# Attention by pairs of heads in half-height matmuls, inside a one-core transformer trunk kernel

## The chip, the cores and the metric

The kernel runs on one NeuronCore of a Trainium2 chip. TensorE (the matrix engine, PE in the profile; its weight loads are the row PEld), VectorE (DVE), ScalarE (ACT), GpSimd (POOL) and SyncE (SP, which issues DMAs) each follow their own instruction stream and wait for one another through semaphores. The metric is the device time of one execution in microseconds (us); lower is better. The program is launched once for the whole layer.

## What is computed

One layer of a streaming encoder over 1024 tokens of width 1024, in f32. What matters here is its middle part:

```python
z = rmsnorm(x) @ w_in                 # 512 columns u, then q, k, v of 512 each
# 8 heads of 64: every chunk of 64 tokens attends to itself and the 8 chunks before
s  = q @ k.T * (1 / 8) + bias[head]   # relative position, clipped; masked outside the band
pr = softmax(s)
o  = pr @ v
a  = pool_mixer(u)                    # trailing means over 2, 4, 8, 16 tokens, a small linear map
h  = x + concat(a, o) @ w_out
```

After that come a gated MLP of width 2816 with a causal depthwise convolution, a gated embedding, and a last norm. They are not touched by the change.

To keep f32 accuracy with the matrix engine's faster f32r type, an operand is split into a high part (rounded to f32r) and a low part (the rest). A product of two split operands is made of three matmuls: high x high, high x low, low x high. `mm3` (L126 to L130) does this; `split` (L132 to L134) makes the two parts with one copy on ScalarE and one subtract on VectorE.

## The kernel before, in words

Tokens stand in eight tiles of 128. A query tile t sees at most five tiles of keys (t - 4 to t), so a tile's score row has 128 to 640 columns. The stages around attention are: a start (norm, first projections of Q and K for heads 0 and 1, values for the first four heads), the attention stage, the output projection, the MLP, the gate.

In the attention stage one instruction stream of TensorE is written out by hand; the other engines' order is made by the scheduler from priorities (`high_priority(AHEAD)` moves something ahead). The main loop (L549 ff.) runs over 64 items i, head by head, tile by tile:

- `scores(i)` (L341): the 64 rows of a head are stacked twice into the array's 128 rows, high and low part, so that two matmuls (L352 and L353 in two column halves for five key tiles, L360 and L361 otherwise) give all four products. VectorE adds the bias and takes the row minimum (scores are kept negated) out of PSUM (L354 or L362), ScalarE takes the exponential with its sum (L364), VectorE the reciprocal (L365), and the scaling goes to ScalarE for every third item (L367) and to VectorE for the rest (L369). Score rows have three buffers `Sb`.
- `probs_t(i - 2)` (L371): the probabilities of two items ago are transposed in blocks of 128x128 (L378) into PSUM banks 6 and 7 and copied out as high part (ScalarE, L385) and low part (VectorE, L386).
- `values(...)` (L392): for a window of two query tiles, up to 12 matmuls of 256 columns against the values (L395, L396), then two instructions that join the two halves (L401, L402).
- Between these come steps of a generator `fill` (`rest`): projections of the other heads' Q and K (`project_qk`), of the remaining values (`project_v`) and of the pooling part (`project_u`), each step three matmuls of 512 columns or six of 256. There are 32 steps for each of three Q/K pairs, 32 for the values and 64 for the pooling part: 192. `fill_room` decides how many steps follow each item from estimates of the other engines' time (`BASE` and more) and of TensorE's, so that `FILL` steps are spread over the loop.
- `project` (L407) loads a block of weights (a DMA by SP), splits it and multiplies at once. Two weight buffers exist (`wring`).
- `qk_stack` (L274 to L292): for each head six instructions per half of 512 tokens put the projected Q and K (`qk32`) into the stacked layout. They go into a list `later`, of which `LATER` run per item.

Of the kernel before, what the change touches and what calls it, by code (L numbers as in the profile page):

```python
# [11 lines left out]
P = 128  # L12
# [52 lines left out]
FILL = 164  # L65
BASE = 2.0
LATER = 3
DRAIN = 4
# [4 lines left out]
def key_tiles(i):  # L73

    return min(i % NTOK + 1, BANDT) if 0 <= i < N_HEADS * NTOK else 0


def fill_room():


    vec_t, pe_t = [], []
    for i in range(N_HEADS * NTOK):
        a, b = key_tiles(i), key_tiles(i - 2)
        vec_t.append(BASE + 0.2 * key_tiles(i - 3) + 0.13 * b)
        pe_t.append(0.11 * a + 0.11 * b + (0.22 * (key_tiles(i - 5) + 1) if i % 2 and i >= 5 else 0.0))
    lo, hi = 0.0, 10.0
    for _ in range(60):
        m = (lo + hi) / 2
        room = [max(0.0, m * v - p) / 0.65 for v, p in zip(vec_t, pe_t)]
        lo, hi = (m, hi) if sum(room) < FILL else (lo, m)  # L90
    return room


def trunk(tc, xT, pT, vecs, w_qk0, w_in, w_v, bias, counts, pool_w, w_out, w_up, w_down,
# [4 lines left out]
    with tc.tile_pool(name="sb", bufs=1) as sb, \  # L99
# [47 lines left out]
        st = [small[:, 56 + 3 * i:59 + 3 * i] for i in range(3)]  # L147
        sa = [small[:, b:b + 3] for b in (24, 27, 30, 33, 66, 69)]
# [7 lines left out]
        stacks = []  # L156
        for s in range(2):
            base = r(96 + 12 * s, 3072).rearrange("p (a t) -> p a t", a=3)
            stacks.append((base[:, 0], base[:, 1], base[:, 2]))
# [6 lines left out]
        biasb = [f(12 + 2.5 * s, 640) for s in range(2)]  # L166
        Sb = [f(b, 640) for b in (17, 19.5, 57.5)]
# [106 lines left out]
        def qk_stack(j):  # L274

            Q1, K1, K2 = stacks[j]
            a = slice(HD * j, HD * j + HD)
            b = slice(HD * (1 - j), HD * (1 - j) + HD)
            q, k = qk32[0], qk32[1]
            todo = []  # L280
            for h in range(2):
                z = slice(h * 512, (h + 1) * 512)
                todo += [
                    lambda z=z: act.activation(Q1[a, z], q[a, z], AF.Copy, scale=-0.125),
                    lambda z=z: dve.scalar_tensor_tensor(Q1[b, z], q[a, z], -0.125, rv(Q1[a, z]),
                                                         ALU.mult, ALU.subtract),
                    lambda z=z: act.activation(K2[a, z], k[a, z], AF.Copy),
                    lambda z=z: dve.tensor_tensor(K2[b, z], k[a, z], rv(K2[a, z]), ALU.subtract),
                    lambda z=z: act.activation(K1[b, z], k[a, z], AF.Copy),
                    lambda z=z: dve.tensor_copy(K1[a, z], rv(K2[b, z])),  # L290
                ]
            return todo  # L292
# [27 lines left out]
        later += qk_stack(0)  # L320
        run_later(len(later))
        later += qk_stack(1)
# [6 lines left out]
        def load_bias(h):  # L329
            b = biasb[h % 2]  # L330
# [5 lines left out]
        def keys(i):  # L336
            t = i % NTOK
            k0 = max(0, t - 4)
            return i // NTOK, t, k0, t + 1 - k0

        def scores(i):  # L341
            h, t, k0, nk = keys(i)
            Q1, K1, K2 = stacks[h % 2]
            b = biasb[h % 2]
            q = Q1[:, t * P:(t + 1) * P]
            S = Sb[i % 3]
            s_ = st[i % 3]
            n, ki = nk * P, k0 * P
            if nk == BANDT:
                for z in range(2):  # L350
                    ks = slice(ki + 320 * z, ki + 320 * z + 320)
                    pe.matmul(PS[:, 4 + z, 0:320], q, K2[:, ks], start=True, stop=False)  # L352
# [54 lines left out]
        def project(ct, evac, heads=0, eng=dve):  # L407
# [6 lines left out]
            for h in range(2):  # L414
# [5 lines left out]
                while stacked[0] < heads:  # L420
                    yield False
# [900 lines left out]
```

## Time and profile before

| | |
|---|---|
| median of 3 runs | 1134.56 us (1134.21 to 1136.07) |
| the profiled execution's own time | 1134.33 us |
| span of its trace | 1132.6 us |
| TensorE busy | 1123.2 us, 5554 matmuls |
| VectorE busy | 889.3 us |
| ScalarE busy | 600.6 us |
| granted TensorE clock | full in all slices |

The span is the time from the first to the last instruction in the trace; the execution's own time has some 1.7 us around it. In a row of a group (line, engine, operation, out<-in, shape, count) the first number behind the bar is the busy time in us, the second the mean duration of one in ns, the third the idle time of the engine just before them with what ended it. A row of the timeline has start and duration in us. Matmul records overlap, since a matmul starts before the one ahead of it has left the array; their distance from start to start tells what each costs in the stream. A row of the wait view names who waited for whom, with the total in us, the times and the longest.

### The profile page before, as it was taken

How to read it: one execution, taken by the hardware profiler on the slowest of the kernel's cores; microseconds unless marked ns; L12 is line 12 of the kernel's file. 1: busy time of each engine (PE TensorE's matmuls, PEld its weight loads, DVE VectorE, ACT ScalarE, POOL GpSimd, SP SyncE). 2: the span in 40 equal slices, each digit the busy share in tenths (PEclk: the TensorE clock that was granted, in tenths of full speed). 3: DMA queues.
4: the chain of work that ended last, by engine and by line, in shares of the span. 5: the costliest groups of instructions: out<-in, count | busy, mean ns of one | idle time of the engine just before them, and what ended most of it. 6: DMA issues, size and time to landing. Idle time of an engine off the chain costs nothing.

```text
span 1132.6 us, 15484 instructions
## 1 busy us (share of the span) xinstructions
PE 1123.2 (99%) x5554; PEld 948.4 (84%) x5554; DVE 889.3 (79%) x1532; ACT 600.6 (53%) x1056; POOL 143.1 (13%) x188
## 2 busy tenths in 40 slices
PE   9999999999999999999999999999999999999997
PEld 7988998888888888888888888888888888888887
DVE  8678878879658888887788788877877789986845
ACT  8568677765654554444444344444444435564634
POOL 0000000074002210120112011201120112000000
PEclk9999999999999999999999999999999999999999
DMA  7010102104500154575557555765576556420003
GB/s 268 38 49 31 50 12 69 40 29 137 189 19 10 61 148 135 142 174 141 145 153 176 140 143 152 162 157 132 152 160 158 144 149 128 151 93 19 1 27 122
DMA packets 64588, 124.81 MB, mean 110 GB/s; under 512 B 7296, under 2 KB 8704, under 8 KB 64512
## 3 DMA queue, kind: packets, MB, share of 16 engines
q1 hardware_dynamic: 50400, 98.33, 25.9%
q0 software_dynamic: 13824, 25.17, 13.9%
q8 instruction: 43, 0.70, 0.2%
q10 hardware_dynamic: 288, 0.33, 0.1%
q14 instruction: 33, 0.27, 0.1%
HBM read 109.13 MB, written 14.68 MB: 109 GB/s over the span
## 4 chain that ended last, share of the span: by engine, by line
PE 91%; DVE 4%; ACT 2%; issue 1%; POOL 1%; DMA 0%; SPq 0%; POOLq 0%; DVEq 0%; ACTq 0%
PE PS L128 28%; PE PS L129 28%; PE PS L130 28%; PE PS L378 2%; PE PS L396 1%; PE PS L395 1%; DVE R L134 1%; PE PS L353 1%; PE PS L352 1%; ACT R L133 0%; PE PS L361 0%; PE PS L360 0%; ACT F L364 0%; DMA F<-in_xT 0%; POOL TB L786 0%
## 5 line engine op out<-in xcount | busy, mean ns | idle before, releaser
L128 PE MATMUL PS<-R 128*128 128x512 f32 (+1 forms) x1136 | 435.1, 383 | 0.0
L130 PE MATMUL PS<-R 128*128 128x512 f32 (+1 forms) x1136 | 430.6, 379 | 0.0
L129 PE MATMUL PS<-R 128*128 128x512 f32 (+1 forms) x1072 | 412.7, 385 | 0.2 <-DVE R L241 0.2
L130 PEld LDWEIGHTS PS<-R 128*128 128x128 f32 x1136 | 213.5, 188 | 40.7
L128 PEld LDWEIGHTS PS<-R 128*128 128x128 f32 x1136 | 213.7, 188 | 38.8 <-ACT R L133 0.5
L133 ACT ACTIVATE R<-F 128x512 fp32r<-128x512 f32 (+2 forms) x225 | 140.6, 637 | 176.2 <-PE PS L129 77.9
L129 PEld LDWEIGHTS PS<-R 128*128 128x128 f32 x1072 | 201.6, 188 | 38.5 <-DVE R L241 1.3
L134 DVE TENSOR_TENSOR R<-F,R 128x512 fp32r<-128x512 f32 (+2 forms) x221 | 152.3, 700 | 46.7 <-ACT R L133 45.5
L1021 DVE TENSOR_TENSOR F<-F,PS 128x512 f32<-128x512 f32 x140 | 92.6, 681 | 6.8 <-PE PS L130 6.6
L133 ACT ACTIVATE BQ<-RW 128x512 fp32r<-128x512 f32 x90 | 52.6, 622 | 81.6 <-PE PS L129 77.6
L711 DVE TENSOR_TENSOR F<-F 128x512 f32<-128x512 f32 x88 | 60.5, 688 | 37.4 <-DMA F<-in_w_up 36.1
L964 POOL DMA_DIRECT2D RW<-Yd x56 | 49.1, 878 | 255.4 <-DMA RW<-Yd 194.5
L964 POOL DMA_DIRECT2D RW<-in_w_down x40 | 35.5, 949 | 236.3 <-DMA RW<-in_w_down 193.9
L134 DVE TENSOR_TENSOR BQ<-RW,BQ 128x512 fp32r<-128x512 f32 x90 | 59.1, 684 | 2.9 <-PE PS L129 2.2
L364 ACT ACTIVATE F<-F,small 128x640 f32<-128x640 f32 (+2 forms) x64 | 44.4, 693 | 21.5 <-DVE small L362 13.4
L129 PE MATMUL PS<-BQ 128*128 128x512 f32 x140 | 54.6, 390 | 0.1
L130 PE MATMUL PS<-BQ 128*128 128x512 f32 x140 | 54.5, 389 | 0.0
L128 PE MATMUL PS<-R,BQ 128*128 128x512 f32 x140 | 54.5, 389 | 0.0
L129 PE MATMUL PS<-R,BQ 128*128 128x512 f32 x140 | 54.5, 389 | 0.0
L130 PE MATMUL PS<-R,BQ 128*128 128x512 f32 x140 | 54.5, 389 | 0.0
L128 PE MATMUL PS<-BQ 128*128 128x512 f32 x140 | 54.5, 389 | 0.0
L847 ACT ACTIVATE F<-F,vec 128x1024 f32<-128x1024 f32 (+1 forms) x25 | 28.6, 1143 | 43.5 <-DVE F L822 37.2
(188 smaller groups left out, 1797.7 us busy)
## 6 DMA issues: line engine op xcount, KB each, us to landing
F<-in_w_up SPq DMA_DIRECT2D x91, 256.0 KB, 3.8
RW<-Yd SPq DMA_DIRECT2D x60, 256.0 KB, 3.6
RW<-Yd POOLq DMA_DIRECT2D x56, 256.0 KB, 4.7
RW<-in_w_down SPq DMA_DIRECT2D x50, 256.0 KB, 2.9
RW<-in_w_down POOLq DMA_DIRECT2D x40, 256.0 KB, 6.2
Yd<-F SPq DMA_DIRECT2D x40, 256.0 KB, 3.5
F<-in_w_in SPq DMA_DIRECT2D x10, 512.0 KB, 3.5
F<-in_xT SPq DMA_DIRECT2D x16, 256.0 KB, 5.8
```

The lines of the kernel that those rows point to most:

```text
L128: pe.matmul(ps, ahi, bhi, start=first, stop=False, skip_group_check=more)
L129: pe.matmul(ps, ahi, blo, start=False, stop=False, skip_group_check=more)
L130: pe.matmul(ps, alo, bhi, start=False, stop=last, skip_group_check=more)
L133: both = (act.activation(hi, src, AF.Copy), dve.tensor_tensor(lo, src, rv(hi), ALU.subtract))
L134: dve.tensor_tensor(lo, src, rv(hi), ALU.subtract))
L352: pe.matmul(PS[:, 4 + z, 0:320], q, K2[:, ks], start=True, stop=False)
L364: act.activation(S[:, 0:n], S[:, 0:n], AF.Exp, bias=s_[:, 0:1], scale=-1.0, accum_out=s_[:, 1:2])
L378: pe.transpose(pst[:, j * P:(j + 1) * P], S[:, j * P:(j + 1) * P], ident)
L711: return dve.tensor_tensor(rawu[to], rawu[a], rawu[b], op)
L847: act.activation(y, Gb[:, 2 + a:2 + b], AF.Identity, bias=vec[:, C_CB + fi:C_CB + fi + 1], scale=cw(2))
L964: pool.dma_start(t, src, accum_op=ALU.add)
L1021: dve.tensor_tensor(t, t, PS[:, 4 + d], ALU.subtract if n in (1, 5) else ALU.add)
```

## The change

The loop runs over 28 units instead of 64 items: for each of four pairs of heads, tiles 0 and 1 together and then each of the tiles 2 to 7. Q and K of a pair are kept in their natural layout, head 2c in partitions 0 to 63 and head 2c + 1 in 64 to 127, with a high and a low array each (`lay` in place of `qk_stack`); K has two buffers, Q one. Scores are matmuls on 64 rows with a `tile_position` of row 0 or 64, alternating between the two heads and writing to different PSUM banks, three products each (the low x low product of before is no longer formed). A transpose of 128x128 becomes two of 64 rows and 64 moving columns, again one in each half of the rows. Both kinds stand directly together in TensorE's order: `probs_t(u - 1)`, then `scores(u)`; then `values(u - 2)` and the steps of `fill`. Score rows have two buffers, one for each head of the pair. The copies of the transposed probabilities are in two parts where a row has more than three key tiles. The softmax scaling is on ScalarE for the odd heads and on VectorE for the even ones. The weights of the next block are loaded and split when the block before is half done (`weights`). The constants of `fill_room` differ. Cut to its core:

```diff
-FILL = 164
-BASE = 2.0
-LATER = 3
-DRAIN = 4
+FILL = 168
+BASE = 3.0
+LATER = 8
+DRAIN = 9
-def key_tiles(i):
-
-    return min(i % NTOK + 1, BANDT) if 0 <= i < N_HEADS * NTOK else 0
+UNITS = [(c, ts) for c in range(N_HEADS // 2) for ts in [(0, 1)] + [(t,) for t in range(2, NTOK)]]
+NU = len(UNITS)
+PER = NU // (N_HEADS // 2)
+
+
+def key_tiles(u):
+
+    return sum(min(t + 1, BANDT) for t in UNITS[u][1]) if 0 <= u < NU else 0
+
+
+def window_keys(u):
+
+    t = UNITS[u][1][-1] if 0 <= u < NU else 0
+    return min(t + 1, 6) if t % 2 else 0
...
-    for i in range(N_HEADS * NTOK):
-        a, b = key_tiles(i), key_tiles(i - 2)
-        vec_t.append(BASE + 0.2 * key_tiles(i - 3) + 0.13 * b)
-        pe_t.append(0.11 * a + 0.11 * b + (0.22 * (key_tiles(i - 5) + 1) if i % 2 and i >= 5 else 0.0))
+    for u in range(NU):
+        vec_t.append(BASE + 0.5 * key_tiles(u))
+        pe_t.append(0.4 + 0.18 * key_tiles(u) + 0.11 * key_tiles(u - 1) + 0.48 * window_keys(u - 2))
...
-        room = [max(0.0, m * v - p) / 0.65 for v, p in zip(vec_t, pe_t)]
+        room = [max(0.0, m * v - p) / 0.68 for v, p in zip(vec_t, pe_t)]
...
-        stacks = []
-        for s in range(2):
-            base = r(96 + 12 * s, 3072).rearrange("p (a t) -> p a t", a=3)
-            stacks.append((base[:, 0], base[:, 1], base[:, 2]))
+        Q = [r(96 + 4 * x, 1024) for x in range(2)]
+        K = [[r(104 + 8 * s + 4 * x, 1024) for x in range(2)] for s in range(2)]
...
-        biasb = [f(12 + 2.5 * s, 640) for s in range(2)]
-        Sb = [f(b, 640) for b in (17, 19.5, 57.5)]
+        biasb = [f(b, 640) for b in (12, 14.5, 57.5)]
+        Sb = [f(b, 640) for b in (17, 19.5)]
...
+        laid = set()
+
+        def lay(c, x, h):
+
+            laid.add((c, x, h))
+            z = slice(h * 512, (h + 1) * 512)
+            src = qk32[x][:, z]
+            if x:
+                hi, lo = [a[:, z] for a in K[c % 2]]
+                return [lambda: act.activation(hi, src, AF.Copy),
+                        lambda: dve.tensor_tensor(lo, src, rv(hi), ALU.subtract)]
+            hi, lo = [a[:, z] for a in Q]
+            return [lambda: act.activation(hi, src, AF.Copy, scale=-0.125),
+                    lambda: dve.scalar_tensor_tensor(lo, src, -0.125, rv(hi), ALU.mult, ALU.subtract)]
...
-        later += qk_stack(0)
+        for h in range(2):
+            for x in range(2):
+                later += lay(0, x, h)
         run_later(len(later))
-        later += qk_stack(1)
...
+        def softmax(x, b, ps, S, s_):
...
+            if x:
...
+        halves = [slice(HD * x, HD * x + HD) for x in range(2)]
+
+        def scores(u):
+
+            c, ts = UNITS[u]
+            Kh, Kl = K[c % 2]
+            todo = []
+            for z, t in enumerate(ts):
+                ki, nk = max(0, t - 4) * P, min(t + 1, BANDT)
+                n = nk * P
+                wide = n // 2 if nk > 3 else max(n, 256)
+                places = [[4 + x + 2 * (z + y) for y in range(2 if nk > 3 else 1)] for x in range(2)]
+                for i, (q, k) in enumerate(((Q[0], Kh), (Q[0], Kl), (Q[1], Kh))):
+                    for y in range(len(places[0])):
+                        for x in range(2):
+                            pe.matmul(PS[:, places[x][y], 0:wide], q[halves[x], t * P:(t + 1) * P],
+                                      k[halves[x], ki + y * wide:ki + (y + 1) * wide], start=i == 0, stop=i == 2,
+                                      tile_position=(HD * x, 0))
+                for x in range(2):
+                    p0 = places[x][0]
+                    ps = PS[:, p0:p0 + 3:2, 0:wide] if nk > 3 else PS[:, p0, 0:n]
+                    todo.append((x, biasb[(2 * c + x) % 3][:, 640 - n:640], ps, Sb[x][:, z * P:z * P + n],
+                                 st[(4 * u + 2 * z + x) % 8]))
+            return todo
+
+        def probs_t(u):
+
+            c, ts = UNITS[u]
+            total = key_tiles(u)
+
+            def place(x, m):
+                if total < 4:
+                    return (6, 320 + HD * m) if x else (2, HD * m)
+                return (4 + 2 * x, 320 + HD * m) if m < 3 else (2, P * x + HD * (m - 3))
+
+            todo = []
+            for x in range(2):
+                for m in range(total):
+                    bank, col = place(x, m)
+                    for y in range(2):
+                        pe.transpose(PS[:, bank + y, col:col + HD], Sb[x][halves[y], m * P:(m + 1) * P],
+                                     ident[halves[y], halves[y]], tile_position=(HD * y, 0))
+                m = 0
+                for t in ts:
+                    nk = min(t + 1, BANDT)
+                    i0 = max(0, t - 4) - (t // 2 * 2 - 4)
+                    parts = [(0, nk)] if total < 4 else [(0, 3), (3, nk)]
+                    for a, b in parts:
+                        bank, col = place(x, m + a)
+                        todo.append((x, t % 2 * P, i0 + a, i0 + b, PS[:, bank:bank + 2, col:col + HD * (b - a)]))
+                    m += nk
+            return todo
+
+        def probs_out(todo):
+            for x, q, a, b, ps in todo:
+                src = ps.rearrange("p a (k q) -> p a k q", q=HD)
+                hi, lo = [PT[x][:, y, a:b, q:q + P].rearrange("p k (a q) -> p a k q", a=2) for y in range(2)]
+                with tc.high_priority(AHEAD):
+                    act.activation(hi, src, AF.Copy)
+                    dve.tensor_tensor(lo, src, rv(hi), ALU.subtract)
+
+        def values(u):
+            c_, ts = UNITS[u]
+            w = ts[-1] // 2
+            if ts[-1] % 2 == 0:
+                return
+            while c_ >= 2 and len(v_ready) < 2 * w + 2:
+                next(fill)
             ks = list(range(max(0, 2 * w - 4), 2 * w + 2))
...
+            for j in range(2):
+                pt = PT[j]
+                O = PS[:, 2 + j, 256:512]
+                for n_, k in enumerate(ks):
+                    idx = k - (2 * w - 4)
+                    pe.matmul(O, V[:, k, 2 * c_ + j], pt[:, 0, idx], start=n_ == 0, stop=False)
+                    pe.matmul(O, V[:, k, 2 * c_ + j], pt[:, 1, idx], start=False, stop=n_ == len(ks) - 1)
...
-        def project(ct, evac, heads=0, eng=dve):
-            hi, lo = wring[nw[0] % 2]
+        blocks_, ready = [8 + 1, 4 + 1, 8 + 2, 4 + 2, None, 8 + 3, 4 + 3, 2, 3, 0, 1], {}
+
+        def weights(ct):
+
+            if ct is None or ct in ready:
+                return
+            hi, lo = ready[ct] = wring[nw[0] % 2]
             nw[0] += 1
             t = load(w_in[ct]).rearrange("p (k c) -> p k c", k=KT)
             for ks in (slice(0, 4), slice(4, 8)):
-                act.activation(hi[:, ks], t[:, ks], AF.Copy)
-                eng.tensor_tensor(lo[:, ks], t[:, ks], rv(hi[:, ks]), ALU.subtract)
+                split(t[:, ks], hi[:, ks], lo[:, ks])
+
+        def project(ct, evac, wait=None):
+            weights(ct)
+            hi, lo = ready[ct]
+            behind = blocks_[blocks_.index(ct) + 1] if ct != blocks_[-1] else None
             for h in range(2):
                 bankn[0] += 1
                 bank = bankn[0] % 2
                 for k in range(KT):
                     mm3(PS[:, bank], hi[:, k], lo[:, k], XTH[h][:, k], XTL[h][:, k], k == 0, k == KT - 1)
+                    if (h, k) == (1, 0):
+                        weights(behind)
                     yield True
-                while stacked[0] < heads:
-                    yield False
-                if heads:
+                if wait:
+                    while not all((wait[0], x, h) in laid for x in wait[1]):
+                        yield False
                     run_later(len(later))
                 with tc.high_priority(AHEAD):
                     evac(h, PS[:, bank])
...
         def project_qk(p):
-            for c in range(2):
-                yield from project(4 + 4 * c + p, lambda h, ps, c=c: qk_evac(p, c, h, ps), 2 * p)
-            qk_ready.add(p)
+
+            for x in (1, 0):
+                def evac(h, ps, x=x):
+                    qk_out(x, h, ps)
+                    qk_ready.append((p, x, h))
+                yield from project(4 + 4 * x + p, evac, (p - 1, (x,)))
...
-            yield from project(g, evac)
+            yield from project(g, evac, (N_HEADS // 2 - 1, (0, 1)) if g < 2 else None)
...
+
+        def lay_due(u):
+
+            for c, x, h in list(qk_ready):
+                if u >= (c - 1) * PER + (0 if x else PER - 1 if h else 2):
+                    qk_ready.remove((c, x, h))
+                    later.extend(lay(c, x, h))
...
+        for h in range(3):
+            load_bias(h)
+        for u in range(NU + 1):
+            if u < NU:
+                c, ts = UNITS[u]
+                for h in range(2 if ts[-1] > 3 else 1):
+                    while not all((c, x, h) in laid for x in range(2)):
...
+                        lay_due(u - 1)
+                if ts[0] in (0, 4):
+                    run_later(len(later))
+            turned_ = probs_t(u - 1) if u else []
+            sums = scores(u) if u < NU else []
+            if u > 1:
+                values(u - 2)
+            with tc.high_priority(AHEAD):
+                for todo in sums:
+                    softmax(*todo)
+            probs_out(turned_)
+            if u < NU:
+                if u % PER == PER - 1:
+                    for h in (2 * c + 3, 2 * c + 4):
+                        if h < N_HEADS:
+                            load_bias(h)
+                lay_due(u)
+                credit += room[u]
+                while credit >= 1 and next(fill, True) is not False:
+                    credit -= 1
+                    lay_due(u)
+                run_later(LATER)
+        for _ in range(DRAIN):
+            next(fill)
+        values(NU - 1)
```

135 lines of the change are left out of this document (14 added, 121 removed).

## The prediction

> **What bounds the kernel now.** I read the page's sums and slices first, then the wait view of TensorE, then the attention stretch alone (42 to 275 us, from the first score matmul to the last value matmul).
>
> ```profile
> span 1132.6 us, 15484 instructions
> PE 1123.2 (99%) x5554; PEld 948.4 (84%) x5554; DVE 889.3 (79%) x1532; ACT 600.6 (53%) x1056; POOL 143.1 (13%) x188
> ```
>
> ```profile
> 42.00:275.00 233.00, 232.03 (x1472) 206.80 (x1471) 188.66 (x452) 163.81 (x346) 34.91 (x62) 1.00 0.14 43
> ```
>
> ```profile
> PE PS L216 <- DVE B L214: 1.5, 1, 1.5
> PE PS L378 <- DVE B L386: 0.8, 2, 0.5
> ```
>
> The second fence gives the stretch, the busy time with count of PE, PEld, DVE, ACT and POOL, the granted clock (1.00), DMA share and rate. TensorE is busy in 232.03 of 233.00 us there, and its named waits come to about 2.6 us in the whole kernel, of which 0.8 us lie at the transposes (L378). VectorE has 188.66 us of work (81%) and ScalarE 163.81 (70%) in the same stretch. So TensorE's own work sets the time; a change is worth what it takes from or adds to TensorE's stream.
>
> A busy time is the wrong price, since the records of successive matmuls overlap. The price is the distance from one start to the next, in TensorE's timeline (start, duration):
>
> ```profile
> 62.58 0.31 PE L352 MATMUL PS<-R 128*128 128x320 f32 x1
> 62.72 0.31 PE L353 MATMUL PS<-R 128*128 128x320 f32 x1
> 62.87 0.31 PE L352 MATMUL PS<-R 128*128 128x320 f32 x1
> 63.02 0.31 PE L353 MATMUL PS<-R 128*128 128x320 f32 x1
> 63.16 0.39 PE L128 MATMUL PS<-R 128*128 128x512 f32 x1
> 63.40 0.40 PE L129 MATMUL PS<-R 128*128 128x512 f32 x1
> 63.63 0.39 PE L130 MATMUL PS<-R 128*128 128x512 f32 x1
> 63.86 0.49 PE L378 MATMUL PS<-ident,F 128*128 128x128 f32 x3
> 64.11 0.48 PE L128 MATMUL PS<-R 128*128 128x512 f32 x1
> 64.42 0.39 PE L129 MATMUL PS<-R 128*128 128x512 f32 x1
> ```
>
> Four 320-column matmuls take 63.16 - 62.58 = 0.58 us, 0.147 each with the rounding. A 512-column one takes 0.23. Three transposes and one 512-column matmul take 64.42 - 63.86 = 0.56; less 0.23 that is 0.11 per transpose. 256 columns take 0.12 (L395 to L396 below); 384 columns I put halfway between 256 and 512, 0.175.
>
> ```profile
> 67.30 0.28 PE L395 MATMUL PS<-B,R 128*128 128x256 f32 x1
> 67.42 0.28 PE L396 MATMUL PS<-B,R 128*128 128x256 f32 x1
> ```
>
> ```profile
> L378 PE MATMUL PS<-ident,F 128*128 128x128 f32 x240 | 37.1, 274 | 1.0 <-DVE B L386 0.8
> L352 PE MATMUL PS<-R 128*128 128x320 f32 x64 | 19.3, 309 | 0.0
> L353 PE MATMUL PS<-R 128*128 128x320 f32 x64 | 19.2, 309 | 0.0
> L361 PE MATMUL PS<-R 128*128 128x256 f32 x16 | 4.5, 282 | 0.0
> L361 PE MATMUL PS<-R 128*128 128x512 f32 x8 | 3.1, 394 | 0.0
> L361 PE MATMUL PS<-R 128*128 128x384 f32 x8 | 2.7, 340 | 0.0
> ```
>
> These are groups by form; L360 has the same counts as L361. Scores now: 128 x 0.147 + 32 x 0.12 + 16 x 0.175 + 16 x 0.23 = 18.8 + 3.8 + 2.8 + 3.7 = 29.1 us. Transposes now: 240 x 0.11 = 26.4 us.
>
> **The change, part by part.**
>
> *Scores.* A head has 64 rows. Before, the array's 128 rows hold high and low part of one head, and two matmuls per stretch of keys give four products. After, three products, each a matmul on 64 rows, with the other head's on the other 64 rows beside it. If the two halves run at once, a pair of heads costs three streams instead of four. Per pair: tiles 0 and 1, 3 x 0.12 each; tile 2, 3 x 0.175; tile 3, 6 x 0.12; tiles 4 to 7, 6 x 0.147 each: 0.36 + 0.36 + 0.53 + 0.72 + 3.53 = 5.50. Four pairs: 22.0 us, a gain of 7.1.
>
> *Transposes.* Each 128x128 transpose becomes two of 64 rows with 64 moving columns, in the two halves at once. Side by side, a pair costs half of 0.11: 13.2 us, a gain of 13.2. Together 20.3 us. The bounds of what the halves cost are those of the rivals: all of this gain, or a loss of 22 to 29 us.
>
> *The switch of the array's form.* Visits: one per unit (7 units x 4 pairs) and one for the last transposes, 29, with a switch in and one out: 58. No row of before shows one. Lower bound zero: a switch removes no work, and TensorE has no slack to give. Upper bound: the array runs empty and the next weight load stands in the open. A 512-column matmul's record is 0.39 long at a distance of 0.23, a tail of 0.16; a load takes 0.19 (row below). That is 0.35.
>
> ```profile
> L128 PEld LDWEIGHTS PS<-R 128*128 128x128 f32 x144 | 27.2, 189 | 1.5
> ```
>
> The nearest row is the one place where TensorE was seen to run empty in this stretch and start again, beside the same group of five in full flow:
>
> ```profile
> 156.85 0.28 PE L130 MATMUL PS<-R 128*128 128x256 f32 x1
> 157.58 0.77 PE L378 MATMUL PS<-ident,F 128*128 128x128 f32 x5 [0.45 <-DVE B L386]
> 158.10 0.36 PE L128 MATMUL PS<-R 128*128 128x256 f32 x1
> ```
>
> ```profile
> 124.38 0.71 PE L378 MATMUL PS<-ident,F 128*128 128x128 f32 x5
> 124.84 0.48 PE L128 MATMUL PS<-R,B 128*128 128x512 f32 x1
> ```
>
> From an empty array the group takes 158.10 - 157.58 = 0.52, in flow 0.46: 0.06 for the restart. Tail plus restart, 0.16 + 0.06 = 0.22 per switch; I take that, 58 x 0.22 = 12.8 us. The Trainium skill, TensorEngine Tiling (Array Packing), Key Properties, says that changing the tiling mode drains TensorE, without a price. By that sentence alone the tail is paid and nothing else: 58 x 0.16 = 9.3 us as an estimate, 3.5 us better than my sum; no run here shows a switch yet.
>
> *Value matmuls* keep their 288 x 0.12 us and only stand one visit later, so that they do not wait for the copies of the newest tile. On TensorE nothing. *Projections*, 192 steps, the same work; unit by unit they fill the room. *Weights split sooner*: the next block's DMA, two copies and two subtracts are issued inside the block before. At the old place TensorE's wait view names no wait for them inside the stretch, so no gain; moved earlier past SP's queue they meet only the bias loads, 8 in the stretch, and no wait on either is on TensorE's list. Zero.
>
> *VectorE and ScalarE.* Stacking Q and K takes six instructions per head and half before, two each of Q and K per pair and half after.
>
> ```profile
> L288 DVE TENSOR_TENSOR R<-F,R 64x512 fp32r<-64x512 f32 x16 | 11.0, 686 | 0.7 <-ACT R L287 0.4
> L290 DVE CAST R<-R 64x512 fp32r<-64x512 f32 x16 | 6.7, 422 | 0.5
> L386 DVE TENSOR_TENSOR B<-PS,B 128x640 fp32r<-128x640 f32 x32 | 26.3, 823 | 5.8 <-ACT B L385 5.3
> L386 DVE TENSOR_TENSOR B<-PS,B 128x128 fp32r<-128x128 f32 x8 | 2.3, 287 | 0.2
> L369 DVE TENSOR_SCALAR F<-F,small 128x640 f32<-128x640 f32 x21 | 12.2, 583 | 0.5
> ```
>
> VectorE: 16 x (0.686 + 0.686 + 0.422) = 28.7 us become 16 x 0.686 = 11.0, 17.7 less. The softmax scaling moves from two thirds to one half on VectorE: about 10 x 0.5 = 5 less. The copies of transposed probabilities go from 64 to 104 (26 per pair); by the rows of 128 and 640 columns one costs 0.15 plus 0.00105 per column, so 40 x 0.15 = 6 more. Net 17 less: 172 us in some 225. ScalarE loses as much stacking as it gains in scaling and copies. Neither becomes the bound. None of this moves the end while TensorE is full.
>
> *New waits.* Transposes of a unit now wait for both heads' softmax of the unit just before (two score buffers instead of three, one unit behind instead of two tiles). Chain from the end of the scores, by the 640-column rows:
>
> ```profile
> L354 DVE CUSTOM_DVE_ANT_0 F<-PS,F 128x640 f32<-128x640 f32 x32 | 26.1, 816 | 2.6 <-PE PS L353 2.3
> L364 ACT ACTIVATE F<-F,small 128x640 f32<-128x640 f32 x32 | 26.5, 827 | 7.7 <-DVE small L354 6.7 <-DVE small L365 0.9
> L364 ACT ACTIVATION_READ_ACCUMULATOR F<-F,small 128x1 f32 x64 | 12.0, 187 | 0.0
> L365 DVE RECIPROCAL small<-small 128x1 f32<-128x1 f32 x64 | 10.3, 161 | 16.5 <-ACT F L364 16.1
> L367 ACT ACTIVATE F<-F,small 128x640 f32<-128x640 f32 x11 | 9.0, 821 | 0.5 <-DVE small L365 0.5
> ```
>
> Two reductions, about 0.9 each with their read-outs, exponential 0.83 + 0.19, reciprocal 0.16, scaling 0.82: 3.8 us, and up to one foreign instruction (0.7 to 0.8) ahead at each hand-over: 5 to 6. Cover: 233 us over 28 units is 8.3, less the visit (0.55 + 0.88 + 0.44): 6.4. It just covers; the short unit (tiles 0 and 1, four softmaxes in a row) has less room. Queued behind a late transpose on TensorE are the next scores, values and projections, all of it. Bounds: nothing, or the rival's price. I put 1.5 us net, a few waits of 0.5 like the two at L378.
>
> *Sum*, against the profiled execution's 1134.33 us (the median of the runs is 1134.56): 1134.3 - 7.1 - 13.2 + 12.8 + 1.5 = 1128.3. I predict 1128.
>
> **The rivals.**
>
> 1. *Switches at their full price*: 58 x 0.35 = 20.3 us eat the whole 20.3; with 1.5 us of waits 1136, anything from 1132 to 1137 for prices from 0.28 up. For it: a load of 0.19 cannot run ahead into a form that the array does not have yet. Against: the restart at 157.58 cost 0.06, not 0.19.
>
> 2. *The halves do not run side by side, so slower.* Place: weight loads inside the visit. The one-column matmuls show what a load costs when nothing else limits:
>
> ```profile
> L256 PEld LDWEIGHTS PS<-small,F x16: 192/192/192, 32.8 to 34.5; 128*128 128x128 f32 x16
> ```
>
> Sixteen starts in 1.7 us, 0.11 each, as much as a whole transpose. If the load of one half may not run under its own half's matmul, each of 156 score pairs grows by 0.11 (17 us) and 240 transpose pairs take 0.11 + 0.055 (39.6 us): 22.0 + 17 + 39.6 = 78.6 instead of 55.5, with switches and waits 1172. If the halves' loads take turns, a pair takes at least 0.22, about 85 us: 1178. It decides from 20.3 - 12.8 - 1.5 = 6 us on, 0.015 us per pair. Against it: in every form here a 189 ns load hides under a matmul of the same rows 120 ns apart. The Trainium skill, TensorE: Matmul & The Clock Gate, The mechanism, says that a load overlaps a running matmul only where the row groups differ; by that rule 1172 would come out. This trace does not agree for full-height matmuls (0.12 apart with 0.19 loads); for half-height ones nothing shows it.
>
> 3. *The softmax chain sticks out at each visit.* At 0.5 us on 28 visits, 14 us instead of 1.5: 1141. It decides from (20.3 - 12.8)/28 = 0.27 us per visit. For it: 5 to 6 us of chain against 6.4 of cover; against: VectorE and ScalarE are 20 to 30% free.
>
> 4. *Switches nearly free* (0 to 0.08 each): 1115 to 1120.
>
> **How the numbers follow.** Forecast (1120 to 1132) 0.48; rival 4 0.07; rival 1 0.18; rival 3 0.12; rival 2 0.15. 0.2% is 2.3 us, about what a measurement can tell from no change. Faster: 0.48 + 0.07 = 0.55; rival 1 lies mostly within: same 0.15; the rest of it with rivals 2 and 3: slower 0.30. The range 1115 to 1142 holds all but rival 2, 0.85 in all; the likeliest's own is 1120 to 1132.
>
> **What would show it.** In the changed trace: pairs of half-height score matmuls starting together, pairs some 0.147 apart at 320 columns, and transpose pairs 0.055 apart; 0.2 us beyond the usual distance where a visit begins and ends; the named waits of TensorE at the transposes below 3 us in all. Wrong if pairs are 0.2 us apart (rival 2), the gaps at the visits' edges reach 0.35 (rival 1), or TensorE waits for the softmax scaling in most units (rival 3).

## The result and the profile after

The changed kernel takes 1145.63 us (median, 1143.91 to 1147.10) against 1135.03 before: a ratio of 1.0092 (95% interval 1.0074 to 1.0110). It is slower by 10.6 us; 1128 was forecast, 1115 to 1142 given as the range.

The page of the changed kernel, its span and busy times:

```profile
span 1142.8 us, 16221 instructions
PE 1119.9 (98%) x5914; PEld 935.8 (82%) x5914; DVE 868.3 (76%) x1530; ACT 590.0 (52%) x1074; POOL 144.8 (13%) x188
```

TensorE has less to do (1119.9 us instead of 1123.2) and VectorE 21 us less, and yet the span is 10.2 us longer. TensorE's wait view says where:

```profile
PE PS L395 <- DVE B L414: 12.1, 10, 2.5
PE PS L223 <- DVE B L221: 1.5, 1, 1.5
PE PS L139 <- DVE B L144: 1.0, 1, 1.0
PE PS L138 <- ACT F L839: 0.8, 1, 0.8
```

Before, the transposes waited 0.8 us in all; now (L395) 12.1 us in ten places, each time until a VectorE subtract (L414) that takes the low part of the transposed probabilities out of PSUM. By the program's order that subtract belongs to the transposes of the unit before, which used the same PSUM columns.

Inside a visit, however, the halves of the array do what was hoped for. TensorE's timeline around the visit at 124 us (start, duration; x16 are eight pairs, x12 six pairs):

```profile
123.57 0.39 PE L139 MATMUL PS<-R,B 128*128 128x512 f32 x1
123.80 0.39 PE L140 MATMUL PS<-R,B 128*128 128x512 f32 x1
124.12 0.71 PE L395 MATMUL PS<-ident,F 64*128 64x64 f32 x16
124.64 1.13 PE L370 MATMUL PS<-R 64*128 64x320 f32 x12
125.70 0.50 PE L138 MATMUL PS<-R,B 128*128 128x512 f32 x1
126.04 0.39 PE L139 MATMUL PS<-R,B 128*128 128x512 f32 x1
```

Eight pairs of transposes take 124.64 - 124.12 = 0.52 us, 0.065 a pair (the single records stand 0.062 apart), where a full-height transpose took 0.11. Six pairs of scores take 6 x 0.147 = 0.88 of the 1.06 us to the next form. The edges show the switches: 0.32 us from the last projection matmul to the first transpose instead of 0.23, 0.18 more than the six pairs need before the first projection matmul, and 0.34 instead of 0.23 behind that one: 0.09 + 0.18 + 0.11, some 0.4 us for the visit.

The whole stretch can be added up from start to start, from the first score matmul to one and the same matmul of the output projection: 246.9 us before, 255.0 after. One thing has to be taken out first. In two stretches of the changed kernel, 3.41 us each, the granted clock (the column behind POOL's busy time) is half; the stretch of before has none:

```profile
175.57:178.98 3.41, 3.41 (x16) 3.22 (x15) 2.48 (x8) 2.65 (x7) 0.00 (x0) 0.50 0.00 0
216.54:219.94 3.40, 3.40 (x18) 2.69 (x16) 2.80 (x12) 2.80 (x10) 0.00 (x0) 0.50 0.01 2
```

What the matmuls that start there lose against their usual distances has its own row. Elsewhere, a distance over 0.3 us beyond the usual one is taken as a wait; what is left beyond the usual distances are the edges.

| | before | after | difference | forecast |
|---|---|---|---|---|
| scores | 29.1 | 21.9 | -7.2 | -7.1 |
| transposes | 26.0 | 14.9 | -11.2 | -13.2 |
| edges (29 visits) | 3.3 | 12.1 | +8.8 | +12.8 |
| waits | 1.2 | 15.6 | +14.4 | +1.5 |
| matmuls at half the clock | 0 | 3.3 | +3.3 | none |
| values, projections | 187.3 | 187.3 | 0 | 0 |
| sum | | | +8.2 | -6.0 |

The rows are rounded. Another 2.0 us come after this stretch (around 418 us a matmul of the MLP waits 0.85 us for ScalarE); they lie in code that is the same in both and were not followed up. So what was priced from TensorE's rows came out within 4 us, one term, the new waits, is wrong by 12.9 us, and the clock, 3.3 us, had no term.

### The profile page after: what moved, and what is told of

Read it like the earlier page. It is cut to its first block, busy times and chain, and to the rows that moved or that the text cites. A ratio compares the mean times of both kernels' runs of the same rounds, so it can differ in the third digit from the quotient of the medians.

```text
span 1142.8 us, 16221 instructions
## 1 busy us (share of the span) xinstructions
PE 1119.9 (98%) x5914; PEld 935.8 (82%) x5914; DVE 868.3 (76%) x1530; ACT 590.0 (52%) x1074; POOL 144.8 (13%) x188
## 4 chain that ended last, share of the span: by engine, by line
PE 84%; DVE 6%; ACT 5%; issue 2%; DMA 1%; POOL 1%; DVEq 0%; POOLq 0%; ACTq 0%
PE PS L138 26%; PE PS L139 26%; PE PS L140 26%; PE PS L370 2%; DVE R L144 2%; PE PS L395 2%; ACT F L348 2%; ACT B L413 1%; DVE B L414 1%; ACT R L143 1%; ACT F L433 1%; DMA F<-in_w_up 1%; PE PS L429 1%; PE PS L430 1%; DVE F L343 1%
## 5 line engine op out<-in xcount | busy, mean ns | idle before, releaser
L143 ACT ACTIVATE R<-F 128x512 fp32r<-128x512 f32 (+2 forms) x235 | 146.7, 636 | 171.8 <-PE PS L139 82.4
L144 DVE TENSOR_TENSOR R<-F,R 128x512 fp32r<-128x512 f32 (+2 forms) x231 | 160.9, 706 | 45.7 <-ACT R L143 41.4
L143 ACT ACTIVATE BQ<-RW 128x512 fp32r<-128x512 f32 x90 | 52.6, 622 | 78.8 <-PE PS L139 75.3
L414 DVE TENSOR_TENSOR B<-PS,B 128x384 fp32r<-128x384 f32 (+2 forms) x104 | 46.1, 460 | 25.0 <-ACT B L413 24.3
L348 ACT ACTIVATE F<-F,small 128x640 f32<-128x640 f32 (+4 forms) x64 | 44.3, 693 | 31.3 <-DVE small L343 26.2
```

Of the source, the lines that this page charges most:

```text
L143: both = (act.activation(hi, src, AF.Copy), dve.tensor_tensor(lo, src, rv(hi), ALU.subtract))
L144: dve.tensor_tensor(lo, src, rv(hi), ALU.subtract))
L348: act.activation(S, S, AF.Exp, bias=s_[:, 0:1], scale=-1.0, accum_out=s_[:, 1:2])
L414: dve.tensor_tensor(lo, src, rv(hi), ALU.subtract)
```

## The experiments

**Which visits wait.** In the changed kernel's trace, the visits that wait for long (0.4 to 2.6 us) all follow a unit with 16 or 24 value matmuls in it. So the first theory, A, blamed the value matmuls: the copies of a unit write the one probability buffer of a head, the value matmuls of the unit before still have to read it, and these now stand behind the visit. B was the softmax standing ahead of the copies in the queues, C too little time in such units in any order.

Run e1, value matmuls ahead of the visit:

```diff
+            if u > 1:
+                values(u - 2)
             turned_ = probs_t(u - 1) if u else []
             sums = scores(u) if u < NU else []
-            if u > 1:
-                values(u - 2)
```

> The value matmuls of unit u - 2 stand ahead of visit u instead of behind it; nothing else is changed. Theory A (the value matmuls hold the copies: the copies of the transposed probabilities write the one probability buffer of a head, which the value matmuls of the unit before must have read, so behind the visit they start up to 2.9 us late, and the next visit's transposes wait for them): TensorE's named waits at the transposes fall from 12 us to under 4, the time from 1145.6 to 1131 to 1137. Theory B (the copies are late because the softmax of both heads goes ahead of them on VectorE and ScalarE): waits and time stay within 2 us of the changed kernel. Theory C (too little time per unit with value matmuls, in any order): the same as B.

1167.31 us, ratio to the kernel before 1.0279 (1.0263 to 1.0294): 22 us worse, which no theory had foreseen. Its waits at the transposes:

```profile
PE PS L395 <- DVE F L434: 12.3, 19, 1.5
PE PS L395 <- DVE F L353: 5.7, 4, 2.2
PE PS L395 <- ACT F L351: 5.6, 5, 1.5
```

The transposes now also wait for the joins of the value matmuls (L434) just ahead of them, and the periods were uneven, 9 to 13 us for units with 16 or 24 value matmuls and 6 to 8 without, as the planner still counted them one unit later. Part of the 22 us is the clock: up to 310 us this trace has 23.9 us at half the clock, the changed kernel's 6.8.

Run e2, copies ahead of the softmax:

```diff
+            probs_out(turned_)
             with tc.high_priority(AHEAD):
                 for todo in sums:
                     softmax(*todo)
-            probs_out(turned_)
```

> The copies of the transposed probabilities are issued ahead of the softmax of the same visit instead of behind it. Theory A: the copies still wait for the value matmuls and now hold up the softmax behind them: the time stays or grows by up to 10 us. Theory B: the waits at the transposes fall to a third, the time by 8 us or more. Theory C: within 2 us.

1156.28 us, 1.0181 (1.0164 to 1.0198). Slower by 10.6: against B; A had allowed up to 10. With 13.7 us at half the clock, some of it is the clock again.

Run e3, both edits:

> Both edits together: value matmuls ahead of the visit and copies ahead of the softmax. Theory A: as with the value matmuls ahead alone, within 2 us, waits under 4 us. Theory B: as with the copies ahead alone, 8 us or more below the changed kernel. Theory C: within 2 us of the changed kernel.

1166.09 us, 1.0271 (1.0256 to 1.0286), no better than e1. The waits under 4 us that A expected in e1 and e3 did not come: they are 26 us in both.

Run e4, more room for units with value matmuls:

```diff
-        vec_t.append(BASE + 0.5 * key_tiles(u))
+        vec_t.append(BASE + 0.5 * key_tiles(u) + 0.2 * window_keys(u - 2))
```

> The planner gives a unit with value matmuls up to 1.6 us more (0.2 per key tile of the window, times the common factor), filled with projection steps taken from the other units; the order inside a unit is unchanged. Theory A and theory C: the waits stand in just those units, so they fall by a half or more, the time to 1134 to 1141. Theory B: the units that lose steps wait instead; the time stays within 2 us of 1145.6.

1138.59 us, 1.0030 (1.0020 to 1.0039): 7 us come back, the waits at the transposes are 6.5 us, and the stretches at half the clock are gone. The time of those units does matter. A and C both say so.

Run e5 takes away what makes copies and value matmuls wait for each other. The value matmuls read other data, so the attention output is left out; work and order are the same otherwise:

```diff
-                    pe.matmul(O, V[:, k, 2 * c_ + j], pt[:, 0, idx], start=n_ == 0, stop=False)
+                    pe.matmul(O, V[:, k, 2 * c_ + j], XTH[0][:, idx, 0:256], start=n_ == 0, stop=False)
```

(and XTL in place of the low part).

> The changed kernel's order and work, but the value matmuls read the x tiles in place of the transposed probabilities (the attention output is left out of the result by that), so nothing makes the copies wait for value matmuls, nor these for copies. Theory A (the copies wait for the value matmuls of the unit before): the waits at the transposes fall from 12 us to under 4, the time to 1128 to 1135. Theory C (VectorE and ScalarE have too little time between two visits, whatever the copies wait for): the waits stay above 8 us, the time above 1140.

1146.89 us, 1.0108 (1.0093 to 1.0123), and the same wait:

```profile
PE PS L395 <- DVE B L414: 12.5, 10, 3.0
```

Theory A falls: without that dependence the time stays within 1.3 us.

Run e6, e1 with the planner put right (`window_keys(u - 1)` in `pe_t`):

> As the run with the value matmuls ahead of the visit, but the planner now counts them in the unit in which they stand, so the periods are even again (they were 11 and 6 us there). Theory A: 1131 to 1137. Theory C, and the reading that value matmuls ahead of the visit simply wait for the same copies earlier: between the changed kernel's 1145.6 and the 1167 of that run.

1157.41 us, 1.0196 (1.0179 to 1.0213). The place of the value matmuls ahead of the visit is worse in itself; the uneven periods, with the half clock that came with them (10.2 us at half the clock are left of 23.9), had cost 10 of e1's 22 us.

Run e7 undoes the third part of the change, the earlier splitting of weights:

```diff
-                    if (h, k) == (1, 0):
-                        weights(behind)
```

> The changed kernel with the weights loaded and split at the start of their own block, as before the change. If splitting sooner does nothing (as predicted): within 2 us of 1145.6. If it puts four more long instructions into the queues of ScalarE and VectorE where copies are due, the time falls by 2 to 5 us; if it hides a load, the time grows by 1 us for each of 10 blocks.

1145.32 us, 1.0095 (1.0080 to 1.0110). No effect, as the prediction had it.

Run e8, e4 with `FILL = 180`:

> The planner with 0.2 more per key tile of a window, as in the run that did so, and 180 projection steps inside the loop instead of 168, so that each unit is 0.3 us longer and fewer steps are left for the end. If the remaining 6.5 us of waits at the transposes come from periods that are too short (theory A and C alike): 1132 to 1137; if the steps that now lack behind the last visit matter more: above 1139.

1135.69 us, 1.0006 (0.9996 to 1.0015): as fast as the kernel before, with 4.9 us of waits at the transposes.

**What stands in the queues.** Since the dependence was not it, I read ScalarE's timeline for the unit before the long wait at 197 us in the changed kernel (start, duration; in brackets the idle time before):

```profile
192.65 0.83 ACT L348 ACTIVATE F<-F,small 128x640 f32<-128x640 f32 x1 [2.90 <-DVE small L343]
193.39 0.18 ACT L348 ACTIVATION_READ_ACCUMULATOR F<-F,small 128x1 f32 x1
193.59 0.38 ACT L433 ACTIVATE F<-PS 64x256 f32<-64x256 f32 x1
194.00 0.88 ACT L413 ACTIVATE B<-PS 128x384 fp32r<-128x384 f32 x2
194.90 0.38 ACT L433 ACTIVATE F<-PS 64x256 f32<-64x256 f32 x1
195.30 0.83 ACT L348 ACTIVATE F<-F,small 128x640 f32<-128x640 f32 x1
196.04 0.19 ACT L348 ACTIVATION_READ_ACCUMULATOR F<-F,small 128x1 f32 x1
196.13 0.62 ACT L143 ACTIVATE R<-F 128x512 fp32r<-128x512 f32 x1
196.65 0.36 ACT L413 ACTIVATE B<-PS 128x256 fp32r<-128x256 f32 x1
196.92 0.62 ACT L143 ACTIVATE R<-F 128x512 fp32r<-128x512 f32 x1
197.44 0.62 ACT L290 ACTIVATE R<-F 128x512 fp32r<-128x512 f32 x1
197.96 0.37 ACT L413 ACTIVATE B<-PS 128x256 fp32r<-128x256 f32 x1
198.22 0.82 ACT L351 ACTIVATE F<-F,small 128x640 f32<-128x640 f32 x1
```

and TensorE's transposes of the visit ahead of it, the first matmul behind that visit, and the transposes of the one that follows; the last line is VectorE's first reduction of the unit's scores:

```profile
189.98 0.84 PE L395 MATMUL PS<-ident,F 64*128 64x64 f32 x20
...
191.69 0.39 PE L429 MATMUL PS<-B,R 128*128 128x256 f32 x1
...
197.23 0.40 PE L395 MATMUL PS<-ident,F 64*128 64x64 f32 x6
199.16 0.65 PE L395 MATMUL PS<-ident,F 64*128 64x64 f32 x14 [1.54 <-DVE B L414]
...
191.78 0.82 DVE L343 CUSTOM_DVE_ANT_0 F<-PS,F 128x640 f32<-128x640 f32 x1 [1.31 <-PE PS L370]
```

ScalarE sits idle for 2.90 us, from the last work of the unit before until the first reduction of this unit's scores; then it works without a gap from 192.65 to 199.04: two exponentials, four copies, two joins, one scaling, and three foreign instructions (two weight splits L143, one K copy L290). The transposes begin at 197.23, stop after six and go on at 199.16. ScalarE is 66% busy in the changed kernel's stage, and late all the same, because all its work of a unit arrives at one moment and is due at one moment.

That leaves two readings. D: the foreign instructions are what is too much. E: the loop itself is too long, from a visit's transposes over its scores, both softmaxes and the copies to the next transposes; foreign work only adds to it. In the visit at 190 us the transposes start at 189.98 and the next ones can finish only from 199.16 on, 9.2 us for a unit that TensorE fills in 7.25.

Run e9, weights split by GpSimd (`pool.tensor_copy`, `pool.tensor_tensor` in place of `split` in `weights`):

> The changed kernel with the projection weights split by GpSimd (copy and subtract) instead of ScalarE and VectorE, 20 instructions of 0.62 and 20 of 0.69 us less in their queues. Theory A has fallen (the waits stayed when the value matmuls read other data). Theory D (in units with value matmuls ScalarE's queue, from the first exponential to the last copy or scaling, is full, and weight splits, Q/K copies and bias preparation in it push the last copies past the next visit): waits at the transposes from 12 to 7 us or less, time 1136 to 1141, unless GpSimd's splits come too late for their block. Theory E (the chain of softmax and copies itself is too long, foreign work falls in its gaps): within 2 us of 1145.6.

1142.29 us, 1.0064 (1.0047 to 1.0081), 3.3 below the changed kernel and between the two expectations. But the waits at the transposes are 11.6 us instead of 12.1:

```profile
PE PS L395 <- DVE B L414: 11.2, 11, 1.6
PE PS L395 <- ACT F L351: 0.4, 1, 0.4
```

At the visits of 87, 103 and 157 us, ahead of which no weights are split, the waits are the same within 0.02 us; at those of 171, 197 and 214 us they are 1.6 us shorter together, and one of 1.5 us has come up a visit later. So foreign work decides at which visit a wait falls, and hardly how much is waited. What this trace lacks are the two stretches at half the clock, which had cost the changed kernel 3.3 us.

Run e10, `AHEAD = 240`:

> The changed kernel with the priority of softmax, copies, joins and evacuations raised from 60 to 240 instructions ahead, so that the scheduler puts foreign work behind them. Theory D: waits at the transposes fall by a third or more, the time to 1136 to 1142, or part of it comes back as waits for weights. Theory E: within 2 us of 1145.6.

1146.21 us, 1.0099 (1.0084 to 1.0114). The order on VectorE is the same as before the edit and that on ScalarE nearly so, so this run decides nothing about D.

Run e11, e8 and e9 together:

> The planner with more room for value matmuls and 180 steps in the loop (1135.7 us), and the weights split by GpSimd. Theory D: the 5 us of waits at the transposes fall to 2, the time to 1129 to 1134, below the kernel before. Theory E: 1134 to 1138.

1134.58 us, 1.0002 (0.9992 to 1.0012), 1.1 below e8 and in E's range, not in D's; 3.8 us of waits at the transposes are left, where D had 2.

Run e12 prices the switch by itself, on e8:

```diff
             turned_ = probs_t(u - 1) if u else []
+            if 0 < u < NU and next(fill, True) is not False:
+                credit -= 1
             sums = scores(u) if u < NU else []
```

> The planner with more room and 180 steps (1135.7 us), with one projection step between a unit's transposes and its scores: 27 more visits of the half-height form, 54 more switches. At the predicted 0.22 us per switch 12 us more: 1147.6; at zero 1135.7; at the full price of 0.35 1154.6. The step gives the copies 0.7 us more before the scores' softmax, so up to 3 us may come back.

1151.11 us, 1.0139 (1.0124 to 1.0154), 15.4 above e8. Its waits at the transposes are 8.9 us instead of 4.9:

```profile
PE PS L395 <- DVE B L414: 6.7, 9, 1.3
PE PS L395 <- ACT F L351: 1.1, 4, 0.5
PE PS L395 <- DVE F L353: 1.1, 1, 1.1
```

So 15.4 - 4.0 = 11.4 us for 54 switches, 0.21 each; the forecast had 0.22. Neither trace has a stretch at half the clock in this stage. The expectation had waits falling, by up to 3 us; that they grow by 4 fits E: transposes and scores lie further apart, and the loop holds both.

**Taking the scores out of the loop.** A unit's scores need neither the softmax nor the copies of the unit before; only the transposes do. Run e13 puts them first in the visit:

```diff
-            turned_ = probs_t(u - 1) if u else []
             sums = scores(u) if u < NU else []
+            turned_ = probs_t(u - 1) if u else []
```

> The changed kernel with a visit's scores ahead of its transposes; nothing else differs. Theory E (a loop from one visit's transposes to the next: transposes, scores, both softmaxes and the copies in line on VectorE and ScalarE, next transposes; in units with value matmuls it is longer than the unit): the scores, 1.06 us, leave the loop, since they need neither the softmax nor the copies of the unit before; waits at the transposes fall from 12 to 5 us or less, time 1133 to 1139. Theory A2 (the copies are held by the value matmuls, by data and by their place in the queue, both together): nothing of that is changed, within 2 us of 1145.6.

1135.54 us, 1.0004 (0.9994 to 1.0014): 10 us gone with two lines exchanged, in the range that E had given. Added up as above, its stretch is 9.2 us shorter than the changed kernel's: 5.7 us are waits, 3.3 us the half clock, of which it has none. E had expected at most 5 us of waits at the transposes; there are still 6.6:

```profile
PE PS L395 <- DVE B L414: 6.6, 6, 1.6
```

The same visit as above, in e13's timeline of TensorE:

```profile
192.09 1.15 PE L370 MATMUL PS<-R 64*128 64x320 f32 x12
193.07 0.34 PE L395 MATMUL PS<-ident,F 64*128 64x64 f32 x6
193.92 0.28 PE L395 MATMUL PS<-ident,F 64*128 64x64 f32 x2 [0.50 <-DVE B L414]
```

and the two ends of ScalarE's row of work ahead of it:

```profile
187.40 0.83 ACT L348 ACTIVATE F<-F,small 128x640 f32<-128x640 f32 x1 [2.67 <-DVE small L343]
...
192.97 0.82 ACT L351 ACTIVATE F<-F,small 128x640 f32<-128x640 f32 x1
```

ScalarE does the same instructions in the same 6.4 us (187.40 to 193.79). But TensorE runs the scores while it finishes, and waits 0.50 instead of 1.54 us. E holds against A2, which had the time unchanged.

Run e15 tests what was left of A, the copies held by data and by queue order together: e2 and e5 in one (again without a valid attention output).

> Value matmuls read the x tiles (the attention output is left out by that) and the copies are issued ahead of the softmax, so neither data nor the queue holds the copies: they can run while the scores do. Theory A2: waits at the transposes under 3 us, time 1129 to 1135. Theory E: the softmax now stands behind the copies, the loop keeps its length but for the part of the copies that runs beside the scores (up to 1 us a unit): 1136 to 1146.

1147.97 us, 1.0121 (1.0097 to 1.0145). A2 had 1129 to 1135, and so A falls for good; E's own range, 1136 to 1146, is missed by 2 us too. The copies are free to run beside the scores, and the softmax behind them is as much later (8 of the waits now end with its scaling, L351). With the dependence taken out, the order of copies and softmax moves the time by about 1 us (e5 to e15); with it, by 10.6 (e2), so the dependence does matter where the copies stand first.

Runs e14 and e16, scores first with e8's room and 180 steps, without and with GpSimd's splits:

> Scores first, with the planner's extra room for value matmuls and 180 steps in the loop (1135.7 us without scores first). Theory E: the last 5 us of waits at the transposes go, 1129 to 1133, below the kernel before. Theory A2: 1134 to 1138.

> Scores first, room, 180 steps, and the weights split by GpSimd. If foreign work still stands in the loop: 1 to 3 us below the same without GpSimd; if nothing is left to wait for: within 1.5 us of it.

e14: 1131.96 us, 0.9970 (0.9958 to 0.9981), 0.3% faster than the kernel before. e16: 1132.50 us, 0.9981 (0.9966 to 0.9995): the weight splits no longer disturb anything. e14's wait view:

```profile
PE PS L395 <- DVE B L414: 2.1, 3, 1.6
PE PS L223 <- DVE B L221: 1.5, 1, 1.5
PE PS L138 <- ACT B L143: 1.5, 1, 1.5
```

The second line stands ahead of the loop and is there before the change too (L216). The other two lie at the loop's end: at the transposes 1.6 us for the last ones, and 1.5 us behind the last value matmuls. Run e17 moves projection steps there:

> Scores first with room, and the projection steps placed otherwise at the end of the loop: two more in the last unit, 176 instead of 180 in the loop's plan, 8 instead of 9 behind the last visit, so that 6 instead of 3 are left behind the last value matmuls. The scores-first run with room had 1.6 us of wait at the last transposes and 1.5 us for the copies behind the last values. If these are cover that lacks at the loop's end: 1129 to 1131; if the four steps are missed inside the loop: within 1.5 us of 1132.

1132.62 us, 0.9975 (0.9964 to 0.9985), no gain. Run e18 is e14 with the weights split at their old place:

> Scores first with room (1132.0 us), weights loaded and split at the start of their own block again. As in the changed kernel the place of the splits should not matter: within 1.5 us. If with fewer waits elsewhere a block now waits for its weights: 2 to 6 us slower.

1131.93 us, 0.9973 (0.9962 to 0.9984). The earlier splitting is worth nothing in either setting.

## Why the prediction was wrong, point by point

- *Scores* (-7.1): right, -7.2, and *transposes* (-13.2): -11.2; a pair costs 0.062 us and not 0.055. The halves run side by side. Rival 2 is out: score pairs stand 0.147 us apart, as full-height matmuls of 320 columns did before, which leaves no room for a load of 0.11 ahead of each. The rule of the Trainium skill (TensorE: Matmul & The Clock Gate, The mechanism), read as no load under a matmul of the same rows, does not agree with this trace for half-height matmuls either (the same section also lets a load into a background weight buffer run ahead).
- *Switches* (12.8 us, 0.22 each): right in the price, 0.19 at the visit of 124 us and 0.21 by e12. The edges of the whole stretch are 12.1 us, but those of before, in which nothing switches, were already 3.3, so that the difference is 8.8. The bound of 0.35 was too high. Rival 4 is out, and so is rival 1's price. Its argument is borne out: at all 58 changes the first load of the new form starts together with its first matmul (within 0.003 us), while in flow a load starts together with the matmul before its own:

```profile
123.58 0.19 PEld L140 LDWEIGHTS PS<-R,B 128*128 128x128 f32 x1
124.12 0.57 PEld L395 LDWEIGHTS PS<-ident,F 64*128 64x128 f32 x16 [0.35 <-DVE B L414]
125.70 0.19 PEld L138 LDWEIGHTS PS<-R,B 128*128 128x128 f32 x1 [0.19 <-issue]
```

- *Value matmuls later* and *weights sooner* (zero): the second is shown twice, by e7 and e18. Of the first it is shown that a place ahead of the visit is worse in this order (e1, e6), and that the dependence which the new place makes is not what is waited for (e5).
- *VectorE and ScalarE do not become the bound*: right as a mean (VectorE 70%, ScalarE 66% busy from 54 to 265 us, row below), and of no use for the question.

```profile
54.00:265.00 211.00, 198.96 (x1632) 168.67 (x1631) 148.13 (x410) 140.00 (x340) 22.10 (x42) 0.98 0.12 36
```

- *New waits* (1.5 us): this is the step that failed; they cost 14.4 us. Both sides of its comparison, a chain of 5 to 6 us under a cover of 6.4, were off. The chain had only the softmax and single foreign instructions in it. In the queue stand with it, on the same two engines, four copies and two joins, with the foreign work 6.4 us without a gap on ScalarE alone; from the first reduction (191.78 us) to the transposes that go on (199.16 us) it is 7.4 us. The cover came from 233 us over 28 units, but the first score matmul of before stands at 54.0 us and not at 42 (row below), which makes 220 us, 7.9 per unit and 6.0 of cover; and the unit at 190 us takes TensorE 7.25 us, of which 5.5 lie behind the visit (191.69 to 197.23). Rival 3 named the place and gave 1141 for it; the waits end with the copies rather than with the scaling, in 10 of 28 visits, of up to 2.65 us.

```profile
L360 PE MATMUL PS<-R x32: 277/310/397, 54.0 to 246.5; 128*128 128x256 f32 x16, 128*128 128x384 f32 x8, 128*128 128x512 f32 x8
```

- *The clock* has no term in the sum, as if it stayed full; 3.3 us of the profiled execution went to half-clock stretches.
- Before the change, a loop of this kind had two items of slack (transposes two items behind, three score buffers). The change took one of them, and the prediction saw that but priced it by the softmax alone. This is read from the program's order; no run gives the second item back.
- A small slip: TensorE's named waits before add up to 2.8 us and not 2.6; nothing hangs on it.

## What to carry to other kernels

Where an engine is 99% busy and others have slack, a change can still lose by a loop: follow one buffer from its writer over every instruction in the readers' in-order queues back to its next writer, and hold the sum against the period, not mean occupancies against 100%. Work of the bounding engine that needs nothing from the loop (here the scores) belongs ahead of the step that closes it. Half-height scores paid their halves in full and half-height transposes nearly so (0.062 us a pair for 0.11), and each change of form cost 0.2 us.

## What the runs showed of the hardware

The granted clock fell to half behind some short waits. In the changed kernel, after the wait of 1.8 us at the visit of 214 us, it was:

```profile
214.00:218.00 4.00, 2.42 (x33) 2.06 (x32) 2.32 (x9) 1.95 (x6) 0.00 (x0) 0.82 0.00 0
218.00:222.00 4.00, 4.00 (x14) 3.16 (x14) 3.99 (x16) 3.95 (x13) 0.00 (x0) 0.76 0.01 2
```

In 3.41 us of this it was 0.50, and matmuls of 512 columns were 0.43 us apart instead of 0.23. The same happened behind the wait of 2.6 us at 171 us (0.79 from 171 to 179 us), and not behind those of 1.8 us at 157 and 1.5 us at 197 us (1.00 in the 8 us from each). So a wait can cost more than its own length: e9 has nearly the same waits as the changed kernel without such a stretch, and is 3.3 us faster. What decides between the two was not tested. The Trainium skill, TensorE: Matmul & The Clock Gate, Part 1, ties the return to half rate to an idle window of about 3.4 us; here shorter waits, with transposes and half-height matmuls around them, were followed by it.
